# Fetched expert rows queued behind weight splits on VectorE, with fewer rows in the gate stage and two small edits ahead of it

## The chip, the core and the metric

The kernel runs on one core of one Trainium2 chip. The metric is the time of one execution in microseconds of the device. A core has a matrix engine (TensorE, PE in the rows), a vector engine (VectorE, DVE), an activation engine (ScalarE, ACT), GpSimd (POOL) and SyncE (SP), and each takes its instructions in the order of its own list. A transfer is issued by SP or POOL and moved by 16 DMA engines that all queues share.

## What is computed

The reference is one transformer layer with a product-key expert layer at its end, then two layers of a second kind. Sequence 512, width 1024, all in float32. The part that matters here is the expert layer (`peer_ffn`): each token chooses 16 of 16,384 experts in each of 8 heads, and an expert is one row of `peer_u` and one of `peer_v`.

```python
x = x + cross_attention(hc, m, w_cq[l], w_ckv[l], w_co[l])
hf = rmsnorm(x, norm_ffn_g[l])
x = x + peer_ffn(hf, w_pq[l], sub_keys[l], peer_u[l], peer_v[l])
...
# peer_ffn, for each chunk of 128 tokens
sc = einsum('thcd,chnd->thcn', q, sub_keys)
vals, idx = top_k(sc, 16)                       # in each half of the key
cand = vals[:, :, 0, :, None] + vals[:, :, 1, None, :]
top_s, top_c = top_k(cand.reshape(128, 8, 256), 16)
g = softmax(top_s, axis=-1)
act = gelu(einsum('td,thkd->thk', hc, peer_u[experts]))
return einsum('thk,thkd->td', g * act, peer_v[experts])
```

## The kernel before

Every matrix product in float32 is made as three passes of PE over a split operand: a weight tile of 1 MB is loaded by SP into `raw` (two buffers), ACT rounds it into `hi` (line 202), and VectorE or GpSimd writes the remainder `lo` (line 203); `raw` is free again when `lo` is written. `weights` (lines 193 to 204) does this, and `split` (lines 206 to 214) does the same for values that are computed, in `hi` on ACT (line 210) and `lo` on VectorE (line 211).

The expert layer handles the 512 tokens in two ways. The first 128 tokens (block 0) go by their own rows: `gathered` fetches, for each of 128 choices, one row of `peer_u` for each token by an indirect transfer that POOL issues (line 785, 512 KB), and VectorE takes the dot product with the token (line 790, with a short read of the accumulator). After 128 dots there is one gelu, and 128 rows of `peer_v` are fetched and added, weighted, into `x[:, 0, :]` (line 796). So there are 256 rows in all, each a fetch and one VectorE instruction. The other 384 tokens go densely over all experts, in groups of 512 experts: activations from `peer_u` (three passes of 384 columns), times a gate matrix G, times `peer_v` (three passes of 512 columns).

The stages are these, in the order of the program:

- `memory` and `cross`: cross attention. `out_proj` (lines 680 to 693) ends it: it adds the product to `x`, normalizes with `rms_block` (lines 360 to 370) and transposes the result.
- `peer`: first `x[1..3]` (the residual of the other three blocks) is stored to DRAM (`xd`). `peer_scores` makes the scores, with the weights' `lo` on GpSimd. `peer_gates` chooses experts and builds G as products of one-hot tiles (VectorE lines 1043 to 1046, PE line 1055), in 24 steps of `n`; in each step it also pulls rows from `gathered` (`N_EARLY` in the first 16 steps, `N_LATE` in the last 8) and pumps 23 steps of `ahead`, which makes the activations of the first 22 groups (88 tiles of 24 passes, lines 250 to 252) and stores them to DRAM as `Ad`.
- the main loop of `peer`: 32 groups, 10 that compute their activations (lines 917 to 919, called new here) and 22 that load them from `Ad` (called back here). A group loads G and, if back, `Ad` (lines 874 and 879), multiplies (line 886), splits into a tile `W`, loads and splits two `peer_v` tiles, and runs 72 passes (lines 902 to 904). After each piece `pull` takes the rows that are due, spread so that the last is taken 12 pulls before the end. The last two groups are back groups and have 6 pulls each. At the start of the last group SP loads `x[1..3]` from `xd` again (line 871).

The rows' buffers are a ring of four in a tile of their own in `peer_gates`, and in the main loop three tiles (`row`) and `x[1..3]`, with `h0` as a seventh once all dots are made. The large tiles (`W`, the split `peer_v`, the gate stage's `stage` and ring) share seven slots.

The order of instructions on an engine is not that of the program text: a scheduler places an instruction when its inputs are there by its own reckoning, and the earlier one in the text first where several are ready. `tc.issue_after(ins)` makes it place the instructions of a block that run on the engine of `ins` behind `ins`.

Of the kernel before, what the change touches and what calls it, by code (L numbers as in the profile page):

```python
# [10 lines left out]
F32 = mybir.dt.float32  # L11
# [22 lines left out]
N_AHEAD = 88  # L34
P_CHOOSE, P_GATES = 4, 23

N_EARLY, N_LATE = 1, 6

R_FINAL, R_G, R_B, R_MIX, R_CROSS, R_MEM, R_FFN = 0, 1, 3, 5, 6, 7, 8
G_CONV, G_SUB = 0, 24  # L40
# [122 lines left out]
class Build:  # L163
# [28 lines left out]
    def weights(self, src, shape, lo_eng=None, both=None):  # L192

        nc = self.nc
        shape = [128] + shape
        raw = self.wp.tile(shape, F32, tag="raw", name=self.nm("raw"))
        if both is None:
            hi, lo = (self.wp.tile(shape, F32R, tag=t, name=self.nm(t)) for t in ("hi", "lo"))
        else:
            hi, lo = both[:, 0], both[:, 1]  # L200
        nc.sync.dma_start(raw, src)
        nc.scalar.activation(hi, raw, AF.Copy)  # L202
        (lo_eng or nc.vector).tensor_tensor(lo, raw, hi.bitcast(F32), op=OP.subtract)  # L203
        return hi, lo

    def split(self, hi, lo, src, scale=None):

        nc = self.nc
        if scale is None:
            nc.scalar.activation(hi, src, AF.Copy)  # L210
            nc.vector.tensor_tensor(lo, src, hi.bitcast(F32), op=OP.subtract)  # L211
        else:
            nc.scalar.activation(hi, src, AF.Copy, scale=scale)
            nc.vector.scalar_tensor_tensor(lo, src, scale, hi.bitcast(F32), op0=OP.mult, op1=OP.subtract)
# [142 lines left out]
        self.nc.sync.dma_start(t, bass.AP(tensor=r.tensor, offset=r.offset + i * D, ap=[[0, 128], [1, D]]))  # L357
        return t

    def rms_block(self, x, g, dst):  # L360

        nc = self.nc
        ssq, rs = self.small([128, 2], "ssq"), self.small([128, 1], "rs")
        for h in range(2):
            c = slice(h * 512, h * 512 + 512)
            nc.scalar.activation(dst[:, c], x[:, c], AF.Square, accum_out=ssq[:, h:h + 1])
        nc.vector.tensor_tensor(ssq[:, 0:1], ssq[:, 0:1], ssq[:, 1:2], op=OP.add)
        self.rstd(rs, ssq[:, 0:1], D, 1e-6)
        part = lambda c: g[c.start // 512] if isinstance(g, list) else g[:, c]
        return lambda c: nc.vector.scalar_tensor_tensor(dst[:, c], x[:, c], rs, part(c), op0=OP.mult, op1=OP.mult)  # L370

# [308 lines left out]
    def out_proj(self, src, X, x, row, keep=None):  # L680

        Xn = self.T_pair()
        with self.tc.tile_pool(name=self.nm("xn"), bufs=2) as p:
            g = self.row(p, row, "g")
            for n in range(2):
                def add(tb, ps):
                    xs = x[:, tb, n * 512:n * 512 + 512]
                    self.nc.vector.tensor_tensor(xs, ps, xs, op=OP.add)
                    if n == 1:
                        t = keep if tb == 0 and keep is not None else p.tile([128, D], F32, tag="xn", name=self.nm("xn"))  # L690
                        self.T_block(t, tb, Xn, self.rms_block(x[:, tb, :], g, t))
                self.tm(src[2 * n:2 * n + 2], X, 4, add, tags=("AABB", "BBBB")[n], whole=(n == 1))
        return Xn

    def memory(self, mT):

        A = self.A
        k = self.big([128, 2, KC, 256], F32R)
        v = self.big([128, 2, 2, D], F32R)
        for u in range(4):  # L700
            W = self.weights(A["w_ck"][u], [8, 256], self.nc.gpsimd if u % 2 else None)
            for nb in range(2):
                self.split(k[:, 0, 2 * u + nb, :], k[:, 1, 2 * u + nb, :], self.fm(W, nb, mT, 256)[:, :256])
        for n in range(2):
            c = slice(n * 512, n * 512 + 512)
            self.tm(A["w_cv"][2 * n:2 * n + 2], mT, 2, lambda tb, ps: self.split(v[:, 0, tb, c], v[:, 1, tb, c], ps))
        return k, v
# [91 lines left out]
    def peer(self, x, hT, h0, op):  # L799
# [29 lines left out]
        with tc.tile_pool(name="act", bufs=3) as ap:  # L829
# [3 lines left out]
            with tc.tile_pool(name="topk1", bufs=2) as p1:  # L833
                self.peer_scores(hT, p1, vals, idx)
            with tc.tile_pool(name="topk2", bufs=2) as p2:
                self.peer_gates(p2, vals, idx, Gd, fill, own, rows)
            for _ in fill:
                pass
            with tc.tile_pool(name="ga", bufs=2) as gp:
# [23 lines left out]
                def pull():  # L863
                    d = due.pop(0)
                    while self.rows_done < 256 and self.rows_done - (256 - left) + 1 <= left * d:
                        next(rows, None)
                        self.rows_done += 1
                for n, q in enumerate(order):
                    if n == len(order) - 1:
# [52 lines left out]
    def peer_scores(self, hT, p, vals, idx):  # L922
        nc, A = self.nc, self.A
        for u in range(8):
            W = self.weights(A["w_pq"][u], [8, 256], nc.gpsimd)
            if u == 0:
                both = self.fm_halves(W, hT)
            sk = p.tile([128, 256], F32, tag="sk", name=self.nm("sk"))
            nc.sync.dma_start(sk, A["sk"][:, u * 256:u * 256 + 256])
            for c in range(2):  # L930
                b = 2 * u + c
                q = p.tile([128, S], F32, tag="q", name=self.nm("q"))
                nc.scalar.activation(q, both[b] if u == 0 else self.fm(W, c, hT), AF.Copy)
                ps = self.ps("C")
                for tb in range(4):
                    nc.tensor.matmul(ps[:, tb * 128:tb * 128 + 128], q[:, tb * 128:tb * 128 + 128],
                                     sk[:, c * 128:c * 128 + 128], start=True, stop=True)
                sc = p.tile([128, 4, 128], F32, tag="sc", name=self.nm("sc"))
                nc.scalar.activation(sc, ps.rearrange("p (a b) -> p a b", b=128), AF.Copy)
                for tb in range(4):  # L940
                    self.top16(sc[:, tb, :], vals[:, tb, b, :], idx[:, tb, b, :])

    def peer_gates(self, p, vals, idx, Gd, fill, own, more):


        nc = self.nc
# [86 lines left out]
        def one_hots(n):  # L1033
# [9 lines left out]
            nc.vector.tensor_tensor(ob, io, col, op=OP.is_equal)  # L1043
            nc.vector.tensor_tensor(oi, io, row, op=OP.is_equal)
            for i, w in enumerate((hi, lo)):
                nc.vector.tensor_tensor(oa[:, i], oi, w, op=OP.mult)
            return oa, ob

        def outer(n, h, oa, ob):
# [18 lines left out]
        for tb in range(2):  # L1068
            for _ in choose(tb):
                pump(P_CHOOSE)  # L1070
        ring = self.big([128, 4, D])
        self.rows_done = 0

        def row_buf():
            return ring[:, self.rows_done % 4]
        self.row_buf = row_buf
        for n in range(0, 48, 2):
            if n % 16 == 0:
                nxt = choose(n // 16 + 2) if n < 32 else iter(())
            hot = [one_hots(n + i) for i in range(2)]  # L1080
            for _ in range(4):
                next(nxt, None)
            if n % 16 == 14:
                for _ in nxt:
                    pass
            for _ in range(N_EARLY if n < 32 else N_LATE):
                next(more)
                self.rows_done += 1
            pump(P_GATES)
            for i in range(2):  # L1090
                for h in range(2):
                    outer(2 * (n + i) + h, h, *hot[i])
# [394 lines left out]
```

## Time and profile before

| | us |
|---|---|
| median of 3 runs | 2863.19 |
| the runs | 2856.2 to 2875.62 |
| the profiled execution | 2859.17 |
| its span, from the first to the last instruction | 2857.4 |

| engine | share of the span that it is busy |
|---|---|
| PE | 95% |
| PE weight load | 80% |
| VectorE | 66% |
| ScalarE | 44% |
| GpSimd | 17% |

Busy time of PE is that of overlapping, pipelined passes, so a stretch in which PE shows as busy can still run at half its clock. The clock that was granted stands beside the busy time in the table of stretches. An engine's wait is put down to the instruction that ended it.

### The profile page before, as it was taken

The page shows a single profiled execution, that of the slowest core. Times are in us where ns is not written, and L with a number is a line of the kernel's source. Part 1 is how long each engine was busy: PE and PEld are TensorE (multiplying, and loading weights), DVE is VectorE, ACT ScalarE, POOL GpSimd, SP SyncE. Part 2 cuts the span into 40 slices and gives each one's busy share as a digit, 9 for nine tenths or more (in the row PEclk, how much of TensorE's full clock was granted, in tenths as well). Part 3 has the DMA queues.
Part 4 walks back from the last instruction along what each step waited for, and adds up shares of the span by engine and source line. Part 5 has one row for each costly group of instructions (what it writes and reads, how often), then busy time and mean ns, then how long its engine had stood idle before and what let it go on. Part 6 is the DMA issues. An engine that isn't in the chain of part 4 may idle for free.

```text
span 2857.4 us, 36004 instructions
## 1 busy us (share of the span) xinstructions
PE 2713.3 (95%) x13725; PEld 2295.6 (80%) x13739; DVE 1886.4 (66%) x3695; ACT 1248.8 (44%) x2066; POOL 485.3 (17%) x320
## 2 busy tenths in 40 slices
PE   8999999999999999888989889999999999999998
PEld 6788888878789999887778777888877778777787
DVE  3546424535579999886788887444548956569665
ACT  4556232334335543333222323333337756367563
POOL 1211000030221134332454552000000000000000
PEclk9999999999999999998999999999999999999999
DMA  5322223242326799999899998545521122221231
GB/s 180 122 81 78 89 89 132 103 148 73 108 86 217 230 338 382 322 333 328 330 339 367 364 349 327 187 177 203 176 100 59 45 92 100 108 74 45 81 111 60
DMA packets 180879, 509.67 MB, mean 178 GB/s; under 512 B 13329, under 2 KB 75025, under 8 KB 158178
## 3 DMA queue, kind: packets, MB, share of 16 engines
q1 hardware_dynamic: 141698, 368.89, 36.5%
q0 software_dynamic: 39008, 138.48, 13.1%
q8 instruction: 108, 1.77, 0.3%
q14 instruction: 65, 0.53, 0.1%
HBM read 456.94 MB, written 54.57 MB: 179 GB/s over the span
## 4 chain that ended last, share of the span: by engine, by line
PE 27%; issue 8%; ACT 5%; DVE 5%; POOL 4%; DMA 1%; POOLq 0%; DVEq 0%; ACTq 0%
POOL big L785 2%; PE psB L282 2%; PE psB L283 2%; PE psB L284 2%; PE psB L903 2%; PE psB L904 2%; PE psA L250 2%; PE psB L902 2%; PE psA L251 2%; PE psA L252 2%; ACT hi L202 1%; POOL row L785 1%; PE psB L331 1%; PE psC L1273 1%; PE psC L902 1%
## 5 line engine op out<-in xcount | busy, mean ns | idle before, releaser
L250 PE MATMUL psA<-big,hi 128*128 128x512 f32 (+1 forms) x1408 | 530.8, 377 | 27.1 <-ACT act L824 11.5
L252 PE MATMUL psA<-big,lo 128*128 128x512 f32 (+1 forms) x1408 | 520.5, 370 | 20.2 <-DVE lo L203 19.9
L202 ACT ACTIVATE hi<-raw 128x2048 fp32r<-128x2048 f32 (+1 forms) x178 | 338.6, 1902 | 455.6 <-PE psA L225 141.6
L203 DVE TENSOR_TENSOR lo<-raw,hi 128x2048 fp32r<-128x2048 f32 (+1 forms) x156 | 353.9, 2269 | 251.2 <-ACT hi L202 250.8
L251 PE MATMUL psA<-big,hi 128*128 128x512 f32 (+1 forms) x1408 | 517.4, 367 | 0.0
L250 PEld LDWEIGHTS psA<-big,hi 128*128 128x128 f32 x1408 | 269.3, 191 | 57.4 <-ACT act L824 14.4
L252 PEld LDWEIGHTS psA<-big,lo 128*128 128x128 f32 x1408 | 269.0, 191 | 52.3 <-DVE lo L203 23.8
L251 PEld LDWEIGHTS psA<-big,hi 128*128 128x128 f32 x1408 | 269.3, 191 | 24.2
L202 ACT ACTIVATE big<-raw 128x2048 fp32r<-128x2048 f32 x64 | 121.7, 1912 | 251.7 <-PE psB L904 244.3
L224 PE MATMUL psA<-big,hi 128*128 128x512 f32 (+1 forms) x560 | 211.7, 378 | 1.7 <-DVE big L211 1.7
L226 PE MATMUL psA<-big,lo 128*128 128x512 f32 (+1 forms) x560 | 211.8, 379 | 1.4 <-POOL lo L203 1.4
L225 PE MATMUL psA<-big,hi 128*128 128x512 f32 (+1 forms) x560 | 211.9, 378 | 0.0
L902 PE MATMUL psB<-big,big 128*128 128x512 f32 x512 | 201.5, 394 | 0.0
L903 PE MATMUL psB<-big,big 128*128 128x512 f32 x512 | 201.1, 393 | 0.0
L904 PE MATMUL psB<-big,big 128*128 128x512 f32 x512 | 200.1, 391 | 0.0
L203 DVE TENSOR_TENSOR big<-raw,big 128x2048 fp32r<-128x2048 f32 x64 | 146.3, 2287 | 79.4 <-ACT big L202 79.4
L785 POOL DMA_INDIRECT big<-in_pu_rows_dram,ids x96 | 134.1, 1397 | 312.5 <-DVE dots L790 178.2
L282 PE MATMUL psB<-hi,big 128*128 128x512 f32 x352 | 138.4, 397 | 2.2 <-ACT big L210 2.2
L283 PE MATMUL psB<-lo,big 128*128 128x512 f32 x352 | 139.3, 396 | 0.0
L284 PE MATMUL psB<-hi,big 128*128 128x512 f32 x352 | 139.3, 396 | 0.0
L790 DVE CUSTOM_DVE_ANT_0 big<-big,h 128x1024 f32<-128x1024 f32 x96 | 115.9, 1220 | 35.3 <-DMA big<-in_pu_rows_dram,ids 35.2
L203 POOL TENSOR_TENSOR lo<-raw,hi 128x2048 fp32r<-128x2048 f32 x22 | 101.2, 4601 | 200.4 <-ACT hi L202 198.1
(340 smaller groups left out, 5520.1 us busy)
## 6 DMA issues: line engine op xcount, KB each, us to landing
raw<-in_pu_dram SPq DMA_DIRECT2D x64, 1024.0 KB, 7.5
raw<-in_pv_dram SPq DMA_DIRECT2D x64, 1024.0 KB, 6.9
raw<-in_w_qk_dram SPq DMA_DIRECT2D x24, 1024.0 KB, 4.8
Gd<-big SPq DMA_DIRECT2D x24, 1024.0 KB, 13.3
ga<-Gd SPq DMA_DIRECT2D x32, 768.0 KB, 7.6
Ad<-act SPq DMA_DIRECT2D x88, 192.0 KB, 6.1
ga<-Ad SPq DMA_DIRECT2D x22, 768.0 KB, 10.1
raw<-in_w_v_dram SPq DMA_DIRECT2D x12, 1024.0 KB, 4.8
```

Of the source, the lines that this page charges most:

```text
L202: nc.scalar.activation(hi, raw, AF.Copy)
L203: (lo_eng or nc.vector).tensor_tensor(lo, raw, hi.bitcast(F32), op=OP.subtract)
L224: nc.tensor.matmul(ps[:, :T], hi[:, k, c], xh[:, k, :T], start=(k == 0), stop=False)
L225: nc.tensor.matmul(ps[:, :T], hi[:, k, c], xl[:, k, :T], start=False, stop=False)
L226: nc.tensor.matmul(ps[:, :T], lo[:, k, c], xh[:, k, :T], start=False, stop=(k == KC - 1))
L250: nc.tensor.matmul(ps, hi[:, k, c], xh[:, k, t0:], start=(k == 0), stop=False)
L251: nc.tensor.matmul(ps, hi[:, k, c], xl[:, k, t0:], start=False, stop=False)
L252: nc.tensor.matmul(ps, lo[:, k, c], xh[:, k, t0:], start=False, stop=(k == KC - 1))
L785: nc.gpsimd.indirect_dma_start(t, None, src, bass.IndirectOffsetOnAxis(ap=own.ids[:, k:k + 1], axis=0))
L902: nc.tensor.matmul(ps, W[:, 0, j4, t], vh[:, j4], start=first, stop=False)
L903: nc.tensor.matmul(ps, W[:, 0, j4, t], vl[:, j4], start=False, stop=False)
L904: nc.tensor.matmul(ps, W[:, 1, j4, t], vh[:, j4], start=False, stop=last)
```

## The change

- Rows in the gate stage: `N_LATE` goes from 6 to 3, so 40 rows instead of 64 are pulled there, and the main loop has 216 instead of 192.
- Their ring: `x[1..3]`, three buffers in the residual's place, instead of four in a tile of their own.
- Their order: `self.last` remembers the last VectorE `lo` of `weights` or `split` (and the last one-hot product), and each pulled row's VectorE instructions are placed behind it. The fetches, which POOL issues, are not tied.
- `rms_block`: the square sum of the first half of a row becomes a function of its own, `rms_first`, which `out_proj` calls when the first half of `x` is final (`n == 0`), into a junk tile. The sum of halves and the scaling become one VectorE instruction.
- `lo` on VectorE instead of GpSimd for two of four key weights in `memory` and for the first two of eight weights in `peer_scores`.

```diff
-N_EARLY, N_LATE = 1, 6
+N_EARLY, N_LATE = 1, 3
...
-        (lo_eng or nc.vector).tensor_tensor(lo, raw, hi.bitcast(F32), op=OP.subtract)
+        last = (lo_eng or nc.vector).tensor_tensor(lo, raw, hi.bitcast(F32), op=OP.subtract)
+        if lo_eng is None:
+            self.last = last
...
-            nc.vector.tensor_tensor(lo, src, hi.bitcast(F32), op=OP.subtract)
+            self.last = nc.vector.tensor_tensor(lo, src, hi.bitcast(F32), op=OP.subtract)
...
-    def rms_block(self, x, g, dst):
-
-        nc = self.nc
-        ssq, rs = self.small([128, 2], "ssq"), self.small([128, 1], "rs")
-        for h in range(2):
-            c = slice(h * 512, h * 512 + 512)
-            nc.scalar.activation(dst[:, c], x[:, c], AF.Square, accum_out=ssq[:, h:h + 1])
-        nc.vector.tensor_tensor(ssq[:, 0:1], ssq[:, 0:1], ssq[:, 1:2], op=OP.add)
-        self.rstd(rs, ssq[:, 0:1], D, 1e-6)
+    def rms_first(self, x, dst, out):
+
+        self.nc.scalar.activation(dst, x[:, :512], AF.Square, accum_out=out)
+        self.nc.vector.tensor_scalar(out, out, 1.0 / D, 1e-6, op0=OP.mult, op1=OP.add)
+        return out
+
+    def rms_block(self, x, g, dst, first=None):
+
+        nc = self.nc
+        ssq, rs, t = self.small([128, 2], "ssq"), self.small([128, 1], "rs"), self.small([128, 1], "rs_t")
+        if first is None:
+            first = self.rms_first(x, dst[:, :512], ssq[:, 0:1])
+        nc.scalar.activation(dst[:, 512:], x[:, 512:], AF.Square, accum_out=ssq[:, 1:2])
+        nc.vector.scalar_tensor_tensor(t, ssq[:, 1:2], 1.0 / D, first, op0=OP.mult, op1=OP.add)
+        nc.gpsimd.tensor_tensor(rs, t, self.mhalf[:, :1], op=OP.pow)
...
+            first = [self.small([128, 1], "first") for _ in range(4)]
...
-                    if n == 1:
+                    if n == 0:
+                        jk = p.tile([128, 512], F32, tag="jk", name=self.nm("jk"))
+                        self.rms_first(x[:, tb, :], jk, first[tb])
+                    else:
...
-                        self.T_block(t, tb, Xn, self.rms_block(x[:, tb, :], g, t))
+                        self.T_block(t, tb, Xn, self.rms_block(x[:, tb, :], g, t, first[tb]))
...
-            W = self.weights(A["w_ck"][u], [8, 256], self.nc.gpsimd if u % 2 else None)
+            W = self.weights(A["w_ck"][u], [8, 256])
...
-                        next(rows, None)
+
+                        with tc.issue_after(self.last.ins):
+                            next(rows, None)
...
-            W = self.weights(A["w_pq"][u], [8, 256], nc.gpsimd)
+            W = self.weights(A["w_pq"][u], [8, 256], nc.gpsimd if u > 1 else None)
...
-                nc.vector.tensor_tensor(oa[:, i], oi, w, op=OP.mult)
+                self.last = nc.vector.tensor_tensor(oa[:, i], oi, w, op=OP.mult)
...
-        ring = self.big([128, 4, D])
         self.rows_done = 0
-
-        def row_buf():
-            return ring[:, self.rows_done % 4]
-        self.row_buf = row_buf
+        self.row_buf = lambda: x[:, 1 + self.rows_done % 3, :]
...
-                next(more)
+                with self.tc.issue_after(self.last.ins):
+                    next(more)
                 self.rows_done += 1
```

## Rows read from the trace of the kernel before

**Rows 1.** Page: busy time of each engine, share of the span, instructions.
```profile
PE 2713.3 (95%) x13725; PEld 2295.6 (80%) x13739; DVE 1886.4 (66%) x3695; ACT 1248.8 (44%) x2066; POOL 485.3 (17%) x320
```

**Rows 2.** Stretches: length; PE, PEld, DVE, ACT, POOL busy; clock; DMA share; GB/s.
```profile
880.00:1180.00 300.00, 282.42 (x1917) 275.10 (x1918) 285.47 (x662) 135.92 (x180) 97.13 (x68) 0.98 0.90 311
1180.00:1313.00 133.00, 118.89 (x824) 116.21 (x823) 100.35 (x136) 48.59 (x68) 43.22 (x34) 0.95 0.92 316
1313.00:1345.00 32.00, 20.78 (x102) 19.89 (x100) 15.72 (x25) 6.42 (x9) 11.69 (x9) 0.81 0.99 362
1345.00:1765.00 420.00, 377.50 (x1661) 315.85 (x1662) 351.03 (x358) 121.22 (x135) 203.96 (x145) 0.95 0.93 351
1765.00:2087.00 322.00, 322.00 (x1509) 277.22 (x1508) 152.04 (x167) 111.50 (x124) 1.68 (x3) 1.00 0.52 187
```

**Rows 3.** Groups on PE, 1765 to 2087: count, busy, mean ns, idle before.
```profile
L917 PE MATMUL psA<-big,hi 128*128 128x384 f32 x128 | 42.8, 334 | 0.0
```

**Rows 4.** Groups on PE, 880 to 1180, with what ended the idle time.
```profile
L250 PE MATMUL psA<-big,hi 128*128 128x384 f32 x465 | 159.4, 343 | 9.9 <-ACT act L824 9.9
L252 PE MATMUL psA<-big,lo 128*128 128x384 f32 x466 | 158.5, 340 | 7.7 <-DVE lo L203 7.6
```

**Rows 5.** Groups on PE, 1180 to 1313, the same columns.
```profile
L250 PE MATMUL psA<-big,hi 128*128 128x384 f32 x189 | 65.7, 347 | 1.6 <-ACT act L824 1.6
L252 PE MATMUL psA<-big,lo 128*128 128x384 f32 x189 | 65.6, 347 | 12.5 <-DVE lo L203 12.3
```

**Rows 6.** Groups of dots on DVE, 880 to 1180 and 1180 to 1313.
```profile
L790 DVE CUSTOM_DVE_ANT_0 big<-big,h 128x1024 f32<-128x1024 f32 x65 | 78.4, 1220 | 14.4 <-DMA big<-in_pu_rows_dram,ids 14.3
L790 DVE CUSTOM_DVE_ANT_0 big<-big,h 128x1024 f32<-128x1024 f32 x31 | 37.5, 1221 | 21.0 <-DMA big<-in_pu_rows_dram,ids 21.0
```

**Rows 7.** Groups on DVE, 1313 to 1765.
```profile
L203 DVE TENSOR_TENSOR big<-raw,big 128x2048 fp32r<-128x2048 f32 x34 | 77.7, 2284 | 1.5 <-ACT big L202 1.5
L796 DVE SCALAR_TENSOR_TENSOR big<-row,dots,big 128x1024 f32<-128x1024 f32 x55 | 70.6, 1283 | 3.5 <-DMA row<-in_pv_dram,ids 2.2
L790 DVE CUSTOM_DVE_ANT_0 row<-row,h 128x1024 f32<-128x1024 f32 x32 | 38.8, 1222 | 39.4 <-DMA row<-in_pu_rows_dram,ids 39.0
L211 DVE TENSOR_TENSOR big<-ga,big 128x384 fp32r<-128x384 f32 x48 | 24.0, 551 | 0.0
```

**Rows 8.** Timeline of DVE from 1507: start, length, instruction, count.
```profile
1510.04 3.92 DVE L796 SCALAR_TENSOR_TENSOR big<-big,dots 128x1024 f32<-128x1024 f32 x3
...
1515.31 2.61 DVE L796 SCALAR_TENSOR_TENSOR big<-row,dots,big 128x1024 f32<-128x1024 f32 x2
```

**Rows 9.** Waits of PE, 1340 to 1770: total, times, longest.
```profile
PE psC L903 <- DVE big L203: 22.8, 9, 4.2
```

**Rows 10.** DMA issues, 1345 to 1765: size, median us from issue to landing.
```profile
raw<-in_pv_dram SPq DMA_DIRECT2D x34, 1024.0 KB, 8.2
ga<-Ad SPq DMA_DIRECT2D x13, 768.0 KB, 12.2
```

**Rows 11.** DMA issues, 1765 to 2087, the same columns.
```profile
raw<-in_pv_dram SPq DMA_DIRECT2D x28, 1024.0 KB, 5.3
ga<-Ad SPq DMA_DIRECT2D x8, 768.0 KB, 6.8
```

**Rows 12.** Page: roundings of the `peer_v` tiles on ACT.
```profile
L202 ACT ACTIVATE big<-raw 128x2048 fp32r<-128x2048 f32 x64 | 121.7, 1912 | 251.7 <-PE psB L904 244.3 <-DVE big L211 5.0 <-PE psA L918 1.9
```

**Rows 13.** Line 785 over the span: time to landing, min, median, max.
```profile
DMA to landing us min/median/max: 4.3/7.8/12.6
```

**Rows 14.** Timeline of DVE and POOL from 1725.
```profile
1725.94 2.28 DVE L203 TENSOR_TENSOR big<-raw,big 128x2048 fp32r<-128x2048 f32 x1
1726.29 2.75 POOL L785 DMA_INDIRECT row<-in_pv_dram,ids  x1 [5.81 <-DVE big L796]
```

**Rows 15.** Waits of PE, 540 to 880: total, times, longest.
```profile
PE psC L350 <- DVE xn L370: 5.8, 5, 3.7
PE psA L238 <- POOL lo L203: 2.2, 1, 2.2
```

More of the change, by code (lines that the diff above doesn't have):

```diff
@@ L835, in peer @@
             with tc.tile_pool(name="topk2", bufs=2) as p2:
-                self.peer_gates(p2, vals, idx, Gd, fill, own, rows)
+                self.peer_gates(p2, vals, idx, Gd, fill, own, rows, x)
             for _ in fill:
@@ L941, in peer_scores, with peer_gates @@
                     self.top16(sc[:, tb, :], vals[:, tb, b, :], idx[:, tb, b, :])
-    def peer_gates(self, p, vals, idx, Gd, fill, own, more):
+    def peer_gates(self, p, vals, idx, Gd, fill, own, more, x):
         nc = self.nc
```

## The prediction

> **What bounds the kernel now.** I read the page first. PE is busy for 95% of the span and no other engine for more than 66% [rows 1], so a gain has to come from where PE waits or runs at half its clock. The page hides that, because the passes are pipelined and their busy time says little. So I read the table of stretches next, for the expert layer, and set the work that PE did in each against its length.
>
> The scale is the stretch 1765 to 2087, where PE is busy throughout at clock 1.00 [rows 2]. Its 1509 passes are 384 of 384 columns (128 on each of three lines [rows 3]) and 1125 of 512, so 723,456 columns in 322 us, or 2247 columns in 1 us. By that scale:
> - 880 to 1180: 1396 passes of 384 columns (465 and 466 on two lines [rows 4], 465 on the third) and 521 of 128, of 1917 in all [rows 2]: 268.3 us of work in 300, 31.7 lost.
> - 1180 to 1313: 568 of 384 (189 on two lines [rows 5], 190 on the third) and 256 of 128: 111.7 in 133, 21.3 lost.
> - 1313 to 1345: 102 of 384: 17.4 in 32, 14.6 lost.
> - 1345 to 1765: 1661 passes; the main loop has 960 of 384 columns (10 new groups of 96), 384 and 96 of them lie in other stretches, so 480 here and 1181 of 512: 351.2 in 420, 68.8 lost.
> - 1765 to 2087: nothing lost.
>
> Together 136 us, all while rows are taken. The losses are waits and their sequel: the granted clock is 0.81 to 0.98 in those stretches, a mixture of 2.4 GHz with spells of 1.2 GHz that follow PE's waits, and 1.00 where there is no wait [rows 2].
>
> What is in the way is VectorE's order. The text pulls 16 rows up to the last eight steps of the gates, but 65 dots were done by 1180 and 96 by 1313 [rows 6]: the scheduler let rows of later steps, and 32 of the main loop, run ahead. VectorE was busy for 285 of the 300 us to 1180 [rows 2]. In the main loop 160 rows are then taken between 1313 and 1765 (the `row` lines of [rows 7] have 87, the other buffers 73), in bunches such as the six between 1510 and 1518 (one is left out of [rows 8]), and a `lo` that PE needs stands behind the bunch: PE's largest wait there is for such a `lo` [rows 9]. Transfers are close to full as well, 351 GB/s at a share of 0.93 [rows 2]; a 1 MB load lands in 8.2 us and `Ad` in 12.2 [rows 10], against 5.3 and 6.8 once no rows are fetched [rows 11].
>
> **The change, part by part.** *Gates.* 40 rows instead of 96 are left ahead of 1313, because rows of the main loop are tied to splits of the main loop. A dot is 1.22 us [rows 6]; with its readback I take 1.3, as three rows in a run take 3.92 [rows 8]. So VectorE sheds 56 x 1.3 = 73 us of 386 in 433 us, and the DMA engines 56 x 0.524 = 29 MB. Of PE's named idle time `lo` ended 7.6 of 17.5 us up to 1180 [rows 4] and 12.3 of 13.9 after it [rows 5]; by these shares of the losses 13.8 + 18.8 = 33 us come back. What stays is the wait for `act`, whose store SP issues. The bounds are 0 and all 53. The ring of three is enough: landing 7.8 [rows 13] and the dot 1.3 make 9.1 us for three rows, and a step has (69 x 384 + 32 x 128) / 2247 = 13.6 us of PE work. At the longest landing, 12.6, it lacks 0.3 us a step, so I cost it at nothing.
>
> *Main loop.* Its floor is 2304 passes of 512 and 960 of 384 columns, 689.1 us; it took 774 (1313 to 2087). The new load on VectorE is 216 rows x 1.29 = 279 us [rows 7], 84 `lo` x 2.29 = 192 and 256 multiplications and splits x 0.5 (24.0 us for 48) = 128: 599 us. So it fits, at 80% of 746. Transfers are 113.2 MB of rows, 88.1 of weights, 42.5 of G and `Ad`, 1.6 of `x`: 245.4 MB, which at PE's pace would be 356 GB/s, slightly over the 351 that the row stretch sustained [rows 2]. So DMA gives one bound: 238 MB outside the last two groups at 351 GB/s, 678 us, the last two groups without rows 144 x 512 / 2247 = 33, and the start 14.6 (its first group waits for G whatever the rows do): 726. The other is the loss beside which rows ran under 0.90 of DMA and a full VectorE, 31.7 on 268.3 up to 1180: 689.1 x 1.118 + 14.6 = 785. I take a third of the way from the first, 746, as VectorE at 80% is nearer the free case than the 95% of that stretch. That is 28 us less than 774.
>
> Why ties should help: `raw` has two buffers, so two loads must turn in the 16.4 us of a back group's 72 passes. Landing 8.2 [rows 10], rounding 1.9 [rows 12] and `lo` 2.3 make 12.4 us; a bunch of six adds 7.9, and 20.3 breaks it. `pull` now gives a back group 216 x 7.2 / 334 = 4.7 rows (the weights of all pulls but the last 12 sum to 334), 2.3 behind each `peer_v` split, which adds 3 us: 15.4, just inside. The fetches are not tied and have six buffers, some 19 us ahead at 3.2 us a row, so a row should have landed when its turn comes.
>
> A fetch can be held up, too: one issued at 1726.29 took 2.75 us and ended at 1729.04, 0.8 us after the split that began before it [rows 14]. The Trainium skill ("SBUF — State Buffer", section "SBUF: two separate sides") says that VectorE and GpSimd share a port pair as an exclusive lock, so that descriptors written by GpSimd wait for certain VectorE instructions to end; this row agrees. By that rule the change puts more fetches beside a 2.3 us split, since each row is now followed by one sooner; with six buffers 7.8 + 2.8 + 1.3 is still under 19 us, so by it the sum stays and only the slower rival below gains a little.
>
> *At the end* SP's reload of `x` waits for the last rows, 12 pulls or 33 us ahead of the last pass. I cost it at nothing; if rows are late by more than that, the last group's loads queue behind it, up to its 16.4 us.
>
> *Ahead of the gates.* The first score weights' `lo` go from GpSimd to VectorE, whose own is 2.3 us; PE waited 2.2 for GpSimd there [rows 15]. The earlier square sum takes an ACT step out of a chain for which PE waited 5.8 in five places [rows 15]; its extra VectorE step replaces another, and it runs beside the other half's passes. I take 4 us of the two together; the bounds are 0 and 8. The four `lo` that move add 9.2 us to VectorE, which is hidden while PE has work and costs up to that if not.
>
> **Sum.** 33 + 28 + 4 = 65 off the profiled execution's own 2859.2 gives 2794. The median of the runs lies 4 above that execution, so I predict 2798.
>
> **Rivals.** (1) The ties do not break up the bunches: VectorE takes the rows as thickly as before, only behind a split, and the loss goes by rows. 83.4 us for 160 rows is 0.52 each; 216 give 113, the loop 802, 28 more than before, so 28 - 33 - 4 = -9 and 2854, within 1%. For it speaks that the scheduler, which goes by its own reckoning, made the bunches; against it that only two or three rows can wait behind one split.
>
> (2) The `raw` turn becomes the bound over the whole loop: rows that ended at 1765 now burden the loads up to the end, and the loss goes by work, 68.8 on 351.2 as between 1345 and 1765. The loop is 689.1 x 1.196 + 14.6 = 839, 65 more, and the last gate steps keep their loss, so only 14 and 4 come back: +47, 2910, slower. It is slower by over 1% from a loop of 821 us on, a turn of 19.2 us, when landing and the wait on VectorE together pass 19.2 - 4.2 = 15 us. Landing 8.2 and the 12.2 of `Ad` [rows 10] speak for it; against it, six rows in a run made that wait and two or three do not.
>
> (3) Nothing is lost: loop 704, gates without loss, 8 ahead: 70 + 53 + 8 = 131, so 2732. Against it is the DMA sum.
>
> **Chances.** The forecast 0.58, (1) 0.18, (2) 0.14 (0.02 of it for the held fetches), (3) 0.10. About 1%, 29 us, is what a measurement of this kernel can tell from no change. Faster by more, under 2834, are the forecast and (3): 0.68; within 1% 0.18; slower 0.14. The range has the forecast's bounds (loop 726 to 785, with the gates' and the early part's ends), the time of (1) with the spread of the runs, and the upper part of (3): 2745 to 2870. It leaves out (2) and the fastest ends, some 0.19.
>
> **What would show it.** In the changed profile: some 40 dots ahead of the first new group's passes, VectorE under 80% in the gates; rows over the whole loop, to about two groups before its end, no more than three or four between two `lo`; the loop near 746 us and the stretch after the last row short; granted clock above 0.97 in it. I am wrong by (1) if bunches of six stay, and by (2) if the clock falls and PE waits for `lo` or `W` up to the end with loads landing in over 10 us.

## The result, and the profile after

The changed kernel takes 2791.18 us, the median of four runs (2790.27 to 2794.88), against 2863.06 for the kernel before beside it: a ratio of 0.9751 with a 95% interval of 0.9719 to 0.9783. The profiled execution took 2790.27, with a span of 2788.5, where the one of before took 2859.17 with 2857.4: 68.9 us less. The forecast was 2798.

The page first: busy time of each engine with its share of the span, beside [rows 1].

```profile
span 2788.5 us, 36022 instructions
PE 2690.5 (96%) x13739; PEld 2278.3 (82%) x13739; DVE 1883.0 (68%) x3699; ACT 1250.9 (45%) x2066; POOL 506.0 (18%) x316
```

Every engine does nearly what it did before, so the page tells only that 69 us of PE's waiting and slow clock are gone. The table of stretches tells where. Its cuts are those of [rows 2] carried over: two for the gates, the bubble ahead of the first `peer_v` pass, then the main loop up to its last dot (1588) and up to its last `peer_v` pass (2026.6). Columns: stretch, length; PE, PEld, DVE, ACT, POOL busy with counts; granted clock; DMA share; GB/s.

```profile
880.00:1180.00 300.00, 295.57 (x2052) 290.41 (x2051) 250.43 (x587) 144.46 (x191) 38.98 (x24) 1.00 0.76 248
1180.00:1274.00 94.00, 94.00 (x689) 92.60 (x688) 72.31 (x93) 40.06 (x57) 37.23 (x23) 1.00 0.98 335
1274.00:1296.00 22.00, 16.85 (x96) 16.21 (x94) 5.77 (x8) 6.08 (x8) 0.48 (x1) 0.97 0.97 338
1296.00:1588.00 292.00, 264.67 (x1149) 220.90 (x1150) 216.88 (x304) 85.07 (x94) 127.90 (x87) 0.93 0.86 318
1588.00:2026.60 438.60, 432.82 (x2023) 371.38 (x2022) 355.49 (x353) 150.71 (x168) 192.09 (x127) 1.00 0.88 337
```

The gates now run at clock 1.00 and are over at 1274, not at 1313. What is left of the loss is in the row with clock 0.93, where dots are taken. With the prediction's scale, 2247 columns in 1 us, each part of a trace has a loss: its length less the time of its columns. I use the same cuts for all kernels below: gates from 880 to the first new group's pass, the start up to the first `peer_v` pass, the dots' part of the loop, and the rest of it.

| us | before | after |
|---|---|---|
| gates from 880: length, loss | 434, 53.5 | 394, 14.9 |
| start: loss | 14.8 | 6.0 |
| loop with dots: length, loss, rows | 81, 16.5, 32 | 292, 46.3, 88 |
| rest of the loop: length, loss, rows | 661, 52.9, 128 | 438, 11.3, 128 |
| whole loop with its start | 773.4 | 752.8 |
| last `peer_v` pass to the end | 770.2 | 761.9 |

The gates end 40.0 us sooner, the loop is 20.6 shorter and what follows it 8.3: 68.9 in all.

In the gates, the groups of dots on VectorE up to 1180 and from there to 1274 (count, busy, mean ns, idle before) answer [rows 6], and PE's waits for `lo` over both (total, times, longest) answer [rows 4, 5]:

```profile
L802 DVE CUSTOM_DVE_ANT_0 big<-big,h 128x1024 f32<-128x1024 f32 x22 | 26.6, 1218 | 0.8 <-DMA big<-in_pu_rows_dram,ids 0.8
L802 DVE CUSTOM_DVE_ANT_0 big<-big,h 128x1024 f32<-128x1024 f32 x18 | 21.3, 1219 | 3.0 <-DMA big<-in_pu_rows_dram,ids 3.0
```

```profile
PE psA L254 <- DVE lo L203: 3.8, 5, 1.3
PE psA L252 <- ACT act L836: 0.5, 1, 0.5
```

There are 40 dots instead of 96. VectorE's idle time in front of dots fell from 35.3 us to 3.8, and PE's for `lo` from 19.9 to 3.8.

In the main loop the waits of VectorE for rows, and those of PE, from 1274 to 2027 (total, times, longest) answer [rows 7, 9]:

```profile
DVE big L802 <- DMA big<-in_pu_rows_dram,ids: 24.0, 6, 7.9
DVE row L802 <- DMA row<-in_pu_rows_dram,ids: 9.4, 3, 4.7
```

```profile
PE psC L917 <- DVE big L203: 19.1, 7, 6.0
PE psC L916 <- ACT big L202: 6.9, 2, 4.9
```

Nine waits for dots' rows remain, 33.4 us, and PE still waits longest for a `lo` of `peer_v`. The sums wait 2.2 us for a row, once in the whole loop. The last row is taken at about 2000, 27 us ahead of the last `peer_v` pass.

### The profile page after: what moved, and what is told of

Read it like the earlier page. It is cut to its first block, busy times and chain, and to the rows that moved or that the text cites. A ratio compares the mean times of both kernels' runs of the same rounds, so it can differ in the third digit from the quotient of the medians.

```text
span 2788.5 us, 36022 instructions
## 1 busy us (share of the span) xinstructions
PE 2690.5 (96%) x13739; PEld 2278.3 (82%) x13739; DVE 1883.0 (68%) x3699; ACT 1250.9 (45%) x2066; POOL 506.0 (18%) x316
## 4 chain that ended last, share of the span: by engine, by line
PE 43%; DVE 13%; issue 8%; ACT 6%; DMA 5%; POOL 2%; POOLq 0%; SPq 0%; DVEq 0%; ACTq 0%
PE psA L252 5%; PE psA L254 5%; PE psA L253 5%; PE psB L286 2%; PE psB L284 2%; PE psB L285 2%; PE psA L226 2%; PE psA L227 2%; DVE lo L203 2%; PE psA L228 2%; DMA raw<-in_pv_dram 2%; PE psB L918 1%; PE psB L333 1%; PE psB L917 1%; PE psB L916 1%
## 5 line engine op out<-in xcount | busy, mean ns | idle before, releaser
L203 DVE TENSOR_TENSOR lo<-raw,hi 128x2048 fp32r<-128x2048 f32 (+1 forms) x160 | 363.3, 2270 | 301.4 <-ACT hi L202 301.1
L252 PEld LDWEIGHTS psA<-big,hi 128*128 128x128 f32 x1408 | 265.7, 189 | 44.1 <-DVE gate L1307 11.3
L253 PEld LDWEIGHTS psA<-big,hi 128*128 128x128 f32 x1408 | 265.7, 189 | 23.7
L226 PEld LDWEIGHTS psA<-big,hi 128*128 128x128 f32 x560 | 105.4, 188 | 23.8 <-DVE big L213 4.5
```

What stands on the lines that cost most here:

```text
L203: last = (lo_eng or nc.vector).tensor_tensor(lo, raw, hi.bitcast(F32), op=OP.subtract)
L226: nc.tensor.matmul(ps[:, :T], hi[:, k, c], xh[:, k, :T], start=(k == 0), stop=False)
L252: nc.tensor.matmul(ps, hi[:, k, c], xh[:, k, t0:], start=(k == 0), stop=False)
L253: nc.tensor.matmul(ps, hi[:, k, c], xl[:, k, t0:], start=False, stop=False)
```

## The experiments

**Without the ties.** The changed kernel, but the scheduler is free to move rows ahead again.

```
-                        with tc.issue_after(self.last.ins):
-                            next(rows, None)
+                        next(rows, None)
...
-                with self.tc.issue_after(self.last.ins):
-                    next(more)
+                next(more)
```

> The changed kernel without the two ties: the rows' VectorE work may run ahead again, all else as changed (40 rows pulled in the gates, ring of three, early edits). If the ties made the gain, as the prediction has it, the gate stage is crowded again, the row stretch ends some 250 us before the loop does, and the time is 2845 to 2862. If fewer rows in the gates and their new ring made it, the time stays at 2790 to 2805.

Measured: 2872.26 us, ratio 1.0027 (1.0015 to 1.004), a little slower than before and 10 us over the range that was expected. 84 dots were done ahead of the loop, 44 of them its own, the gates lost 72.3 us, and the loop took 779.6. The table of stretches, for the end of the loop, shows POOL with three instructions and PE without loss:

```profile
1820.00:2112.00 292.00, 292.00 (x1376) 252.32 (x1375) 141.11 (x155) 101.11 (x113) 1.67 (x3) 1.00 0.54 192
```

So the rows are again over long before the loop is, as in the last stretch of [rows 2]. The smaller `N_LATE`, the ring and the early edits together gain nothing without the ties; the ties are necessary.

**No tie in the gates only.** The second of the two edits above, alone.

> The changed kernel with the tie in the main loop alone; the 40 rows of the gates may be taken whenever they have landed. If it is the main loop's tie that keeps the main loop's rows out of the gates, the gates still hold 40 dots and the time is 2790 to 2797. If the gates' own tie matters, because rows stand ahead of the one-hot products, the gates take 10 us or more longer and the time is 2800 or over.

Measured: 2810.03 us, 0.9801 (0.9776 to 0.9826), some 14 us more than the changed kernel by the ratios, and 19 by the medians. Its loop is that of the changed kernel, 752.4, its gates lose 32.5 instead of 14.9, and the same 40 dots lie ahead of the loop. So the tie in the gates is worth some 14 to 19 us even where no row can leave them: it is the place among the steps that counts there, not only the number of rows.

**The ties alone.** The kernel before with both ties, with `N_LATE` at 6, the ring of four and without the early edits.

```
-                        next(rows, None)
+                        with tc.issue_after(self.last.ins):
+                            next(rows, None)
...
-                next(more)
+                with self.tc.issue_after(self.last.ins):
+                    next(more)
```

> The kernel before with the two ties and nothing else: 64 rows in the gates, six in each of the last eight steps, ring of four. If the ties make the gain, 2795 to 2815: the last eight gate steps hold 6 rows, 7.9 us of VectorE each beside 5.5 us of one-hot products and 3.3 us of a lo, over the 13.6 us of PE work, which gives back up to 25 us, and the main loop has 24 rows fewer, which gains some 10. If the number of rows in the gates makes it, 2845 or over.

Measured: 2821.39 us, 0.9831 (0.9792 to 0.9869), between the two forecasts. The loop has 192 rows and takes 739.0, 34 less than before; the gates keep their loss, 51.8. So the ties carry the loop's gain by themselves, and do nothing for the gates while these have 64 rows. The expectation had it the other way round, some 25 us from the gates and 10 from the loop.

**Six rows in a late step of the changed kernel.** One number.

```
-N_EARLY, N_LATE = 1, 3
+N_EARLY, N_LATE = 1, 6
```

> The changed kernel with six rows instead of three in each of the last eight gate steps, both ties, the ring of three and the early edits kept. If six tied rows in a step crowd VectorE there, as the kernel with ties alone suggests, the gates end some 35 us later (near 1305 instead of 1268), the loop with 192 rows takes some 739, and the time is 2808 to 2820. If it was the ring of four in its own tile or the missing early edits that kept the gates long there, the gates end near 1275 and the time is 2785 or less.

Measured: 2821.71 us, 0.9843 (0.9811 to 0.9875), with 59.5 us lost in the gates and a loop of 741.3 with 194 rows: the ties alone over again, though the ring and the early edits are those of the changed kernel. It is just over the 2808 to 2820 of the first forecast: the gates end at 1317, not near 1305. The table of stretches from 1180 to 1305, and VectorE's and PE's waits from 1180 to 1310, show how the gates lose:

```profile
1180.00:1305.00 125.00, 97.16 (x612) 93.75 (x611) 92.89 (x134) 35.76 (x49) 49.77 (x37) 0.86 0.90 301
```

```profile
DVE big L802 <- DMA big<-in_pu_rows_dram,ids: 31.4, 17, 5.8
PE psA L254 <- DVE lo L203: 26.3, 5, 12.5
```

VectorE is busy for 92.9 of 125 us, 74%, and yet 42.6 of the 59.5 us are lost here, at a clock of 0.86. It isn't full: 17 times it stands at a dot whose row has not landed, 31.4 us in all, with what PE needs behind it in its order, and PE waits 26.3 us for five `lo`.

**Ring of four.** The gates' rows go to a ring of their own again.

```
+        ring = self.big([128, 4, D])
...
-        self.row_buf = lambda: x[:, 1 + self.rows_done % 3, :]
+        def row_buf():
+            return ring[:, self.rows_done % 4]
+        self.row_buf = row_buf
```

> The changed kernel with the gates' ring of four in a tile of its own, as before, instead of three buffers in the residual's place; three rows per late step and both ties kept. The prediction costs the ring of three at nothing: 2788 to 2795. If the slot that the ring gives up is what lets the gates run (a third stage buffer), the gates end 10 us or more later and the time is 2800 or over; if a fourth buffer is missed, 2785 or less.

Measured: 2799.85 us, 0.9777 (0.9758 to 0.9797). In its profile the gates lose 15.1 us, the loop takes 751.6 and the span is 2789.5, all within 1.2 us of the changed kernel; the other runs lie up to 13 us above that execution. The median lies between the two forecasts, a hair under the 2800 of the second, but its gates end no later. No gain from a fourth buffer, as the prediction costed it; whether it costs a few us was not settled.

**The early edits alone.** The kernel before with the edits of the square sums and of the weights' `lo` (in `memory` and in the scores) only.

> The kernel before with the edits to the normalization and to the weights' lo alone. By the prediction's sum 4 us: 2859, with the expert layer as before. A rival that puts the 8 us which the two later layers gained down to the new form of the normalization: 2851, with the stretch from the last expert pass to the end at 762 us instead of 770.

Measured: 2859.4 us, 0.9977 (0.9962 to 0.9992): 4.8 us less than before, with an interval of some 2 to 11, where the prediction had 4. Its profiled execution issues the first load of `peer_u` at 817.5 instead of 821.2. The part behind the loop takes 768.1 us there, so the rival with 762 is not borne out.

**No rows in the loop.** What the loop costs without its 216 rows.

```
-                        with tc.issue_after(self.last.ins):
-                            next(rows, None)
+                        pass
```

> The changed kernel without the 216 rows of the main loop: neither fetched nor taken, so block 0 lacks their part. The loop should then run at its floor of 689 us and the start of some 6: 695 to 700, and the whole at 2735. If the loop stays above 715, something other than the rows holds it, the turn of the raw buffers or the loads of G and Ad.

Measured in a single run: 2737.59 us. The loop in the table of stretches:

```profile
1272.80:1968.00 695.20, 692.53 (x3267) 599.50 (x3266) 325.21 (x356) 239.89 (x266) 1.67 (x3) 1.00 0.55 194
```

695.2 us against a floor of 689.1, at clock 1.00: the loop's loads, roundings and `lo` hide beside PE by themselves. All the rest of the changed kernel's 752.8, 58 us, comes with the rows.

**A seventh buffer for the dots.** The loop's ring gets `x`'s first block from the start; before, `h0` joined only when the dots were over. `x`'s first block goes to DRAM and is loaded back ahead of the sums.

```
-        xd = self.dp.tile([3, 128, D], F32, name="xd")
-        for tb in range(1, 4):
-            nc.sync.dma_start(xd[tb - 1], x[:, tb, :])
+        xd = self.dp.tile([4, 128, D], F32, name="xd")
+        for tb in (1, 2, 3, 0):
+            nc.sync.dma_start(xd[(tb - 1) % 4], x[:, tb, :])
...
-                ring += [x[:, tb, :] for tb in range(1, 4)]
+                ring += [x[:, tb, :] for tb in (1, 2, 3, 0)]
...
-                        ring.append(h0)
+                        nc.sync.dma_start(x[:, 0, :], xd[3])
+                        ring[6] = h0
```

> The changed kernel with a seventh row buffer in the main loop while dots are taken: x[0] lends its place, after its store to DRAM, and is loaded again before the first weighted sum, when h0 takes its turn as the seventh. The dots' part lost most of what the main loop still loses, and VectorE waits there for fetched rows (33 us in nine waits) while with seven buffers in the sums' part it waits 2. If buffers are what is short, the loop falls from 753 to some 735 to 745 and the time to 2775 to 2785. If the thick bunch of rows behind the splits of a new group is to blame, whatever the buffers, 2788 to 2795.

Measured: 2787.09 us, 0.9738 (0.9714 to 0.9761); the changed kernel's own interval covers that. In the profile the loop takes 741.9 us, as expected if buffers are short, but the time lies between the two forecasts. The dots' part loses 32.8 us instead of 46.3, the rest 13.6 instead of 11.3, and VectorE waits 23.8 us for dots' rows instead of 33.4.

**Sixteen rows more in the gates.** `N_EARLY` 2 instead of 1, so 56 dots lie ahead of the loop and 200 rows in it.

> The changed kernel with two rows instead of one in each of the first 16 gate steps, so 56 rows in the gates and 200 in the main loop. VectorE is busy for 250 of 300 us up to 1180 in the changed kernel, and 16 more rows are 21 us. By the price of a row in the main loop that the kernel with ties alone gives against the changed one (739 for 192 rows, 753 for 216, so 0.57 us a row) the loop gains 9, the gates lose 0 to 5: 2782 to 2788. If the gates' PE work is what these rows delay again, as six rows per late step did, 2795 to 2805.

Measured: 2793.0 us, 0.9748 (0.9728 to 0.9767): no gain. The gates lose 18.5 instead of 14.9, and the loop is 3.7 shorter; its dots' part loses 29.4 instead of 46.3, but the rest 25.0 instead of 11.3. The expectation that the loop would give more than the gates take was wrong.

**Rows moved to other pulls, and both together.** The due weights of a new group change so that its first four pulls, around the activations, take most of its rows; the next kernel adds the seventh buffer to it. The changed kernel itself ran again on the same chip.

```
-                due = [p for q in order for p in ([1.9] * 10 if q >= na else [1.2] * 6)]
+                due = [p for q in order for p in ([3.1] * 4 + [1.1] * 6 if q >= na else [1.2] * 6)]
```

> The changed kernel as it is, so that the next two are compared on one chip: 2788 to 2795.

> The changed kernel with the rows of a new group moved inside it: weights 3.1 for the four pulls behind its activation pieces and 1.1 for the six behind its expert passes, instead of 1.9 for all ten, so that about two rows stand behind each activation split and some two instead of four behind each peer_v split; the sum per group is the same. If the loop's remaining stalls come from rows that stand in a bunch ahead of the next peer_v lo, the loop falls from 753 to 735 to 745 and the time to 2773 to 2785. If it is the landing of fetched rows, whatever their place, 2787 to 2796.

> The seventh buffer while dots are taken and the moved rows of the run beside it, together. If both act on separate stalls, the seventh buffer's 11 us of the loop and the moved rows' add up: 2765 to 2778. If both touch the same stalls, 2778 to 2788.

Measured: 2794.99 us for the changed kernel (2788.72 to 2801.76; 0.9756, 0.9728 to 0.9783), 2785.94 with the other weights (0.9722, 0.9697 to 0.9747), and 2778.37 with both (2776.53 to 2786.18; 0.9707, 0.9682 to 0.9732), which is the fastest of all. The runs of the last don't overlap those of the first; those of the middle one do. With the other weights alone the loop takes 751.1 us where the changed kernel, run again, has 757.1: the dots' part loses 35.2 instead of 49.9, but the rest 20.9 instead of 12.5. That is neither of the two forecasts for it. With both edits the main loop is 739.1 us, the time falls where the two forecasts meet, and the table of stretches for the dots' part reads:

```profile
1295.00:1572.00 277.00, 258.23 (x1159) 215.88 (x1160) 216.81 (x303) 85.78 (x94) 125.16 (x85) 0.97 0.88 334
```

The clock is 0.97 where it was 0.93, and the loss 28.3 where the changed kernel has 46.3 and, run again, 49.9. VectorE waits 13.4 us for dots' rows. The rest loses 15.7.

## Why the prediction was right, point by point

**The sum.** 2794 was forecast for the profiled execution, 2790.3 came. By terms: gates 33, of which the loss shows 38.6; loop 28, which gave 20.6; early edits 4, which alone measured 4.8 but have 1.4 left in this pair of profiles (the gates end 40.0 us sooner, 38.6 of it by their own loss). The 8.3 us after the loop were in no term. So the total is right partly by luck: the loop gave 7 less and the early edits 3 less, the gates 6 more and the part behind the loop 8 more than the sum had.

**Gates: the size right, the reason not.** The step "VectorE sheds 73 us of 386" took VectorE's occupancy as the reason: 285 of 300 us [rows 2]. VectorE did become less busy, 82% from 880 to 1274 (the text had said under 80%). But the kernel with six late rows loses more than before with VectorE at 74%, because a dot stands at the head of its order while its row is on the way. [rows 6] had shown the same wait, 35.3 us of idle time in front of dots, and the text read it only as a sign that rows ran ahead. [rows 2] had shown it too: from 1180 to 1313 VectorE was busy for only 75%, and 21.3 of 133 us were lost, a larger share than the 31.7 of 300 at 95%. What `N_LATE` 3 and the tie do is let a row land before its turn: 3.8 us of such waits are left. The two work together: three rows without a tie lose 32.5 us in the gates, six rows with one 51.8 or 59.5, three rows with it 14.9. The prediction gave both together one price by PE's waits, and so did not need to tell them apart.

The ring of three at nothing: right within what the two profiles show.

**The start, 14.6 taken as staying:** it fell from 14.8 to 6.0. The text held that the first group waits for G whatever the rows do. But the kernels without a tie in the loop have 14.8 (no ties) and 15.0 (early edits), and all with one have 4.4 to 7.8; the two kernels without a tie in the gates differ by the loop's tie alone, 14.8 and 4.4. So it is the loop's rows, run ahead of the loop, that made the bubble. VectorE's timeline shows how, first before and then in the changed kernel:

```profile
1336.94 1.23 DVE L790 CUSTOM_DVE_ANT_0 row<-row,h 128x1024 f32<-128x1024 f32 x1 [5.42 <-DMA row<-in_pu_rows_dram,ids]
...
1340.12 1.23 DVE L790 CUSTOM_DVE_ANT_0 row<-row,h 128x1024 f32<-128x1024 f32 x1 [1.95 <-DMA row<-in_pu_rows_dram,ids]
...
1341.27 1.02 DVE L886 TENSOR_TENSOR act<-act,ga 128x384 f32<-128x384 f32 x2
```

```profile
1292.40 1.03 DVE L900 TENSOR_TENSOR act<-act,ga 128x384 f32<-128x384 f32 x2 [14.36 <-DMA ga<-Gd]
```

The last line of each is the multiplication by G. By the semaphores in the traces, G had landed at 1335.31 before and at 1292.18 after, 7.7 and 6.4 us after its issue. Before, VectorE stood at dots whose rows had not landed, and multiplied 6.0 us after G was there; in the changed kernel it does so 0.2 us after. So most of the bubble came from VectorE's order, and little from the transfer of G.

**The loop: right in its direction, mis-sized in its first part.** 752.8 us came and 757.1 the second time, for a forecast of 746. The bounds 726 and 785 hold it. The clock over the loop is 0.97, as a mean of 0.93 and 1.00. The loss is not even:
- The sums' part lost 11.3 us on 128 rows, 0.09 us a row, where before they cost 52.9, 0.41 a row.
- The dots' part lost 46.3 on 88 rows, 0.53 a row, as large as the 0.52 of rival (1).

So the forecast is right for the sums, and rival (1) has its price in the dots, though not by its mechanism, as the next points show. The step that failed there is "the fetches have six buffers, some 19 us ahead, so a row should have landed when its turn comes". The timeline of VectorE (start, length, instruction, idle time before it) shows one of the nine waits. This is a part of it; three dots behind the wait and the small steps between are left out:

```profile
1392.91 2.28 DVE L203 TENSOR_TENSOR big<-raw,big 128x2048 fp32r<-128x2048 f32 x1
...
1395.58 1.22 DVE L802 CUSTOM_DVE_ANT_0 big<-big,h 128x1024 f32<-128x1024 f32 x1
...
1397.20 1.22 DVE L802 CUSTOM_DVE_ANT_0 big<-big,h 128x1024 f32<-128x1024 f32 x1
...
1398.81 1.21 DVE L802 CUSTOM_DVE_ANT_0 row<-row,h 128x1024 f32<-128x1024 f32 x1
...
1399.95 1.22 DVE L802 CUSTOM_DVE_ANT_0 row<-row,h 128x1024 f32<-128x1024 f32 x1
...
1409.06 1.23 DVE L802 CUSTOM_DVE_ANT_0 big<-big,h 128x1024 f32<-128x1024 f32 x1 [7.88 <-DMA big<-in_pu_rows_dram,ids]
...
1415.53 2.28 DVE L203 TENSOR_TENSOR big<-raw,big 128x2048 fp32r<-128x2048 f32 x1
```

Four dots run in 6 us, the fifth stands for 7.9 until its row lands, three more follow, and only then comes the `lo` at 1415.53. What it needs was there ten us earlier, as ACT's timeline shows:

```profile
1403.48 1.92 ACT L202 ACTIVATE big<-raw 128x2048 fp32r<-128x2048 f32 x1 [5.64 <-PE psB L918]
```

Its `hi` ended at 1405.40. The table of stretches for the same time shows how full the DMA engines were:

```profile
1392.00:1395.00 3.00, 1.58 (x6) 0.67 (x4) 3.00 (x4) 0.91 (x2) 1.01 (x1) 1.00 0.50 154
1404.00:1407.00 3.00, 3.00 (x15) 2.49 (x14) 0.00 (x0) 1.39 (x1) 0.00 (x0) 1.00 1.02 419
```

The DMA engines are half idle ahead of the four dots, and full while VectorE waits. GpSimd's timeline has the fetches that those dots set off:

```profile
1397.88 1.34 POOL L797 DMA_INDIRECT big<-in_pu_rows_dram,ids  x1 [4.08 <-DVE act L900]
1399.53 1.31 POOL L797 DMA_INDIRECT big<-in_pu_rows_dram,ids  x1 [0.30 <-issue]
1401.14 0.94 POOL L797 DMA_INDIRECT row<-in_pu_rows_dram,ids  x1 [0.30 <-issue]
1402.39 0.93 POOL L797 DMA_INDIRECT row<-in_pu_rows_dram,ids  x1 [0.30 <-issue]
```

The semaphores in the trace tell which fetch a dot waits for. The row of the fifth dot comes with the first of these four, issued at 1397.88; it landed at 1409.04, 11.2 us later. Behind this dot stand the dots of two rows that were fetched earlier, at 1387.10 and 1392.79, and had landed at 1392.52 and 1397.06. So VectorE doesn't take the rows in the order of their fetches. The ties hold the dots and not the fetches, and the two orders come apart: with fetches and dots matched in this way, 27 of the loop's 88 dots stand ahead of one whose row was fetched earlier. In the three kernels without a tie in the loop, no dot of the loop does. In seven of the nine waits, 29.6 us of the 33.4, a row that had landed stands behind the one that had not, and the row whose turn it would have been by the order of the fetches was there when the wait began.

So the estimate of 19 us ahead fails by the order above all: it holds for rows that are taken as they were fetched. It also takes rows as evenly spaced, and they are not. The four dots free their buffers together, so four fetches start within 5 us and share the engines with the loads beside them; that this lengthens them is my reading and not shown. Fetches land no later in the dots' part than in the sums' part, 8.4 us after their issue against 8.7 in the median, and the sums wait for a row only once. Each sum adds to the same `x[:, 0, :]`, so the sums follow one another in the program's order.

A buffer more (46.3 to 32.8) and other pulls (49.9 to 35.2, on the same chip) each took part of the loss of the dots' part, and both together 21.6 us of it; the rest of the loop gave some of that back. With the other pulls 12 dots instead of 27 stand ahead of an earlier row. That the row waits are a cause of the loss is shown so far, and by the trace that most of them come from the order; a kernel with dots in the order of the fetches was not run.

**"No more than three or four rows between two `lo`": wrong.** Counted from VectorE's order, there are up to eight in the changed kernel, and seven or eight in nine places, as there were up to eight before. What the ties changed is how the rows are spread: before, 160 rows stood in front of 35 of the 84 `lo`, 4.6 each, and none in front of the other 49; now 216 stand in front of 71, 3.0 each. The prediction's own sign of rival (1), bunches of six that stay, thus came. But six of the bunches of eight lie in the sums' part, and PE waited for one of the `lo` behind them, 0.2 us; it did for three of the four bunches of six to eight in the dots' part, 12.3 us. The kernel with other weights has bunches of up to eleven and still loses less in the dots' part. So the argument by which I held the ties to help, a raw turn of 12.4 us broken by 7.9 more, does not decide alone: a bunch of eight is harmless where the rows have landed.

**The rivals.** (1), the loss goes by rows: not so for the loop as a whole, 802 forecast and 752.8 found; without ties it is nearly that (rows over by 1820, 779.6 with 172 rows). (2), the raw turn bounds the whole loop: fell, since the part from 1588 to the loop's end ran at clock 1.00 with 5.8 us of PE's time idle, and the loop without rows took 695.2. (3), nothing is lost: only there, and in the gates nearly.

**What stays open.** The part behind the loop took 770.2 us before and 761.9 after, and of the change only the new form of `rms_block` lies in it, in the norm that opens it. The changed kernel again had 765.5, the early edits alone, which have that form too, 768.1, the ties alone 768.2, and without ties 762.3. Two executions of the same kernel are 3.6 apart there, so part of the 8.3 is chance; whether the rest comes from the order of the work was not tried. Nor is it settled why seven buffers leave 33 us of loss with dots and 11 with sums, though the order of the dots is a likely part of it. What the last 28 us of the kernel with both edits are is open as well; of the transfers in its loop, VectorE waits longest for `Ad`, 26.4 us in nine. Why the gates without ties and with three late rows lose more (72.3) than those of before (53.5) was not separated either.

## What to carry to other kernels

Where one in-order engine serves both the path that sets the end and a side stream fed by transfers, ask of each side step not how long it runs but whether its data is there when it comes to the head of the order: an engine at 74% lost more here than one at 95%. A scheduler that takes whatever seems ready will run the side stream ahead and spend it early; tying each side step behind a step of the main path spread it over the whole loop, and with that came the gain, though the largest bunches stayed. Look for the rest where one engine starts the transfers and another uses them: if only the second is tied, check in the trace that both keep the same order, because a step whose data is there can stand behind one whose data is not.

## What the runs showed of the hardware

In the part with dots the transfers come in waves: 154 GB/s in three us and 419 some ten us later, at a mean of 318 over the 292 us. The sums' part has a higher mean, 337 GB/s at a share of 0.88, and waits for a row once, 2.2 us. So the mean share of a stretch did not tell whether rows arrive in time.

A fetch keeps GpSimd longer beside dots than beside sums. The groups of line 797 up to 1590 and behind it (count, min, median, max in ns, first and last start):

```profile
L797 POOL DMA_INDIRECT row<-in_pu_rows_dram,ids x41: 934/1312/3052, 1295.5 to 1569.0; - x41
L797 POOL DMA_INDIRECT row<-in_pv_dram,ids x51: 934/1017/4072, 1603.6 to 1974.5; - x51
```

The medians are 0.3 us apart and the longest are 3 to 4 us. What runs on VectorE when a fetch starts bears on its length: in the changed kernel 25 fetches without any VectorE instruction beside them took 0.93 to 0.94 us, and all 47 that start during a `lo` of 2.28 us end 0.81 to 0.84 us after it. The Trainium skill ("SBUF — State Buffer", section "SBUF: two separate sides") describes a lock on a pair of ports that would do this: a VectorE instruction with two SBUF inputs holds it against a GpSimd one that reads SBUF. The rows agree, since a `lo` has two such inputs and a fetch reads its row numbers from SBUF. No run here shows what this costs the kernel; such lengths are too small to make a wait of 7.9 us by themselves.

The same kernel, run twice, differed by 8 us in its profiled span (2788.5 and 2796.5), 4.3 of it in the main loop (752.8 and 757.1). Differences of that size between the variants above, such as that of the ring of four, carry no weight by themselves.
